# Value projections of two head groups in one 512-column product, half-block scores, and conditioning products in four column groups of the array, in a two-layer hybrid backbone

## The chip, the cores and the metric

The kernel runs on one core of one Trainium2 chip. The metric is the time of one execution on the device, in microseconds (us). A profiled execution of the same kernel gives the trace from which all rows below are taken.

## What is computed

The reference has two layers over 512 latent tokens (and 256 context tokens) of width 1024; all of it is in float32.

```python
m = silu(cvec) @ ada_w + ada_b                      # shift, scale, gate, 1024 each
h = rmsnorm(x) * (1 + scale) + shift                # the same for the context with c_ctx
# layer 0: bidirectional gated linear recurrence, 16 heads of key and value width 128
q, v, zf, zb, gate = split(h @ w_in, 5)             # 2048 columns each
f = lb + (1 - lb) * sigmoid(z); g = log f; k = 1 - f   # forward and backward
S_t = diag(exp g_t) S_{t-1} + k_t^T v_t ; o_t = S_t^T silu(q_t)   # chunks of 16 tokens
x = x + gate_ada * ((rmsnorm(o_f + o_b) * silu(gate)) @ w_out)
# layer 1: gated convolution along the rows of the token grid, norm, gate, projection, final rmsnorm
```

Within a chunk of 16 tokens, and between the chunks of a block of 128 tokens, the output comes from masked scores q k^T (times decay factors) that are multiplied with v; between blocks it comes from states S.

## The kernel before, in words

All activations lie transposed in SBUF (features on partitions). Most products are made precise by a split: each float32 operand becomes a high part and a low part of type fp32r (`split`, L134: ScalarE rounds the high part, VectorE or GpSimd subtracts for the low part), and hi*hi, lo*hi and hi*lo are summed in PSUM, three products for one. Products whose operands are left in plain float32 are issued as two records each, so one float32 matmul is two PE records in the trace.

**Conditioning.** `ada_start` (L144 to L166) makes the shift and scale columns in four steps jj of 512 columns. The stationary operand is the conditioning vector, 2 columns (latent and context) or 4 (high and low), and the 512 weight columns move. `ADA_SPLIT` says which weight pieces are split first (L152 to L156) and which are used in plain float32 (L150). The result, a row of 2 or 4 partitions, is copied (L158) and transposed back into columns by four small products with `sel` (L161). Its weight pieces have six buffers (L230). Between the steps the first five weight pieces of layer 0 are multiplied ("early" products, L248 to L254).

**Layer 0** (L574 to L653) goes over eight groups gi of two heads. For each group TensorE makes forget-gate products (`proj_z`: pz for 512 latent and pc for 256 context tokens, two directions, two heads), query products (pq), value products (pv), output-gate products (pg), and in groups 2, 3 and 5 output products of finished heads (op). A weight piece is 512 KB; its high and low parts have three buffers (L208), and a piece of a buffer that is still read waits for it on ScalarE and VectorE.

`proj_values` (L562) takes two pieces of 256 columns for the two heads of a group. `proj_v` (L307) multiplies them with 6 token tiles (four latent, two context): the tokens are stationary (128 columns), the 256 weight columns move, 8 steps of k with three products each, so 144 records in a group. They stand between the query and the gate products (L582); in the last group between the query products and the recurrence (L595).

`gla` (L329) is the recurrence of one head. Its first part (to the first `yield`, L435) has the gates, running sums, context states (h_ct, h_s, which needs the values), the scaled queries and keys qh and kh, and the block states S. Its second part (L438 to L492) makes the scores: three levels of distance (L439: operands ql and kl on VectorE, then for each of the four 128-token blocks one 128 x 128 float32 product, L465, and one masked copy of 128 x 512 into a1, L466) and two diagonal products (L467 to L475, a1 and a2). So a head has 20 score matmuls and five masked copies. `A` (L477) is their sum; the output products (L484 to L492) follow in one run, and `readout` normalizes. The qh, kh, S tiles have one buffer each, so that heads follow each other there; sg (the gates), qs and gs have two.

**The order** on each engine is chosen when the program is built, by a planner that walks the instructions in program order and fills each engine by estimated times; the chip then runs each engine's list strictly in that order. In the trace the recurrence of a group stands between the forget-gate and query products of the next group.

**Layer 1** (L656 on) has its own products and pools. It shares the weight buffers with layer 0.

Of the kernel before, what the change touches and what calls it, by code (L numbers as in the profile page):

```python
# [9 lines left out]
F32 = mybir.dt.float32  # L10
F32R = mybir.dt.float32r
# [5 lines left out]
P = 128  # L17
D = 1024
KD = D // P
L = 512  # L20
# [15 lines left out]
ADA_SPLIT = ((1, 1, 1, 1), (1, 0, 2, 1), (1, 0, 2, 1), (1, 1, 0, 0))  # L36
# [3 lines left out]
LAST_KQ = 1  # L40
FINAL = ((0, 2, 1), (2, 4, 0), (4, 6, 0))
# [11 lines left out]
C_END = C_TAP + P  # L53
# [7 lines left out]
def hybrid_kernel(ctx: ExitStack, tc: tile.TileContext, xT, ctxT, cvec, consts, norm_g, ada_b, ada_a, ada_c,  # L61
# [63 lines left out]
    sc4 = cpool.tile([P, KD, 4], F32R, name="sc4")  # L125
    V.tensor_copy(out=sc4[:, :, 0:2], in_=sc)
    V.tensor_tensor(out=sc4[:, :, 2:4], in0=sc, in1=sc4[:, :, 0:2].bitcast(F32), op=ALU.subtract)
# [16 lines left out]
    def ada_start(jj, raws, pool, sel):  # L144
        ps = ps_m.tile([P, 512], F32, name=f"adaps{jj}", tag="ms")
        n = 4 if ADA_SPLIT[jj][0] else 2
        for kk, raw in enumerate(raws):
            if not ADA_SPLIT[jj][kk]:
                for k in range(2):
                    mm(ps[0:2], lhsT=sc[:, 2 * kk + k, :], rhs=raw[:, k, :], start=(kk == 0 and k == 0), stop=(kk == 3 and k == 1))  # L150
                continue
            hi, lo = split(pool, raw, [2, 512], f"ada{jj}_{kk}", V if ADA_SPLIT[jj][kk] == 1 else G, ("ahi", "alo"), 2)  # L152
            for k in range(2):
                mm(ps[0:4], lhsT=sc4[:, 2 * kk + k, :], rhs=hi[:, k, :], start=(kk == 0 and k == 0), stop=False)
            for k in range(2):
                mm(ps[0:2], lhsT=sc4[:, 2 * kk + k, 0:2], rhs=lo[:, k, :], start=False, stop=(kk == 3 and k == 1))  # L156
        row = pool.tile([4, 512], F32, name=f"adarow{jj}", tag="adarow", bufs=2)
        V.tensor_copy(out=row[0:n], in_=ps[0:n])  # L158
        pt_ = ps_m.tile([P, 512], F32, name=f"adat{jj}", tag="ms")
        for i in range(4):  # L160
            mm(pt_[:, 2 * i:2 * i + 2], lhsT=row[0:n, i * P:(i + 1) * P], rhs=sel[0:n], start=True, stop=True)  # L161
# [43 lines left out]
    def wpiece(src, shape, name, lo_eng, hi_eng=None):  # L205
        raw = wpool.tile([P] + shape, F32, name=f"{name}_raw", tag="raw")
        nc.sync.dma_start(out=raw, in_=src)
        return split(wpool, raw, shape, name, lo_eng, ("whi", "wlo"), 3, hi_eng)  # L208


    with l0:
# [8 lines left out]
        with tc.tile_pool(name="pinit", bufs=1) as pi:  # L220
            mk = pi.tile([P, 5, P], F32, name="mk")
            eye = pi.tile([4, 4], F32, name="eye")
            nc.gpsimd.dma_start(out=eye, in_=consts[0:4, C_IDN:C_IDN + 4])
            sel = pi.tile([4, 2], F32, name="sel")
            V.tensor_tensor(out=sel, in0=eye[:, 0:2], in1=eye[:, 2:4], op=ALU.add)
# [3 lines left out]
            for jj in range(4):  # L229
                araws.append([pi.tile([P, 2, 512], F32, name=f"ada{jj}_{kk}", tag="araw", bufs=6) for kk in range(4)])  # L230
# [25 lines left out]
            for jj in range(4):  # L256
                ada_start(jj, araws[jj], pi, sel)
# [6 lines left out]
                for i in range(len(early), min(EARLY, len(early) + EARLY_LOADS[jj])):  # L264
                    pool, tags, bufs = (wpool, ("whi", "wlo"), 3) if i < 3 else (pi, ("ehi", "elo"), EARLY - 3)
# [41 lines left out]
        def proj_v(ws, lhi, llo, t, name):  # L307
            ps = ps_p.tile([P, 512], F32, name=name, tag="pj")
            c = slice(t * P, (t + 1) * P)
            for k in range(KD):  # L310
                hi, lo = ws[k // 4]
                mm(ps[:, :256], lhsT=lhi[k][:, c], rhs=hi[:, k % 4, :], start=(k == 0), stop=False)  # L312
                mm(ps[:, :256], lhsT=llo[k][:, c], rhs=hi[:, k % 4, :], start=False, stop=False)  # L313
            for k in range(KD):
                hi, lo = ws[k // 4]
                mm(ps[:, :256], lhsT=lhi[k][:, c], rhs=lo[:, k % 4, :], start=False, stop=(k == KD - 1))
# [12 lines left out]
        def gla(h, j, sg, qs, v):  # L329
# [109 lines left out]
            for lev in (2, 1, 0):  # L439
# [3 lines left out]
                kl = pt.tile([P, L], F32, name=f"{n}_kl{lev}", tag="lk", bufs=2)  # L443
# [4 lines left out]
                else:  # L448
                    ql = pt.tile([P, L], F32, name=f"{n}_ql{lev}", tag="lq", bufs=2)
                    for half in range(2):  # L450
                        dd = [[2 * w, ng_], [CH, hf], [1, CH]]
                        fd = [[2 * hf, ng_], [1, hf], [0, CH]]
                        o, fo = half * w, half * hf + lev * NCH
                        V.tensor_tensor(out=cut(ql, o, dd), in0=cut(qh, o + (1 - half) * L, dd), in1=cut(fac, fo + (1 - half) * 128, fd),
                                        op=ALU.mult)
                        V.tensor_tensor(out=cut(kl, o, dd), in0=cut(kh, o + half * L, dd), in1=cut(fac, 256 + fo + half * 128, fd),
                                        op=ALU.mult)
                p_ = ps_s.tile([P, 512], F32, name=f"{n}_sc{lev}", tag="sc")
                for b in range(NB):
                    bs = slice(b * P, (b + 1) * P)  # L460
                    if lev == 0:
                        qq = cut(qh, L + b * P, [[2 * CH, 4], [CH - L, 2], [1, CH]])
                    else:
                        qq = ql[:, bs]
                    mm(p_[:, bs], lhsT=kl[:, bs], rhs=qq, start=True, stop=True)  # L465
# [108 lines left out]
        for gi in range(8):  # L574
# [4 lines left out]
            if gi < 7:  # L579
# [4 lines left out]
                if gi in OUT_SETS:  # L584
                    out_proj(OUT_SETS[gi])
# [347 lines left out]
```

## Time and profile before

| | us |
|---|---|
| median of 3 runs (lowest, highest) | 1362.88 (1358.25, 1363.73) |
| the profiled execution's own time | 1360.55 |
| its span, first to last instruction | 1358.5 |
| PE busy in the span | 1319.3 |
| VectorE (DVE) busy | 947.6 |
| ScalarE (ACT) busy | 617.5 |
| GpSimd (POOL) busy | 320.1 |

The profiled execution has 2.05 us outside its span. PE's busy time counts each matmul from its start to a modelled end; matmuls overlap, so what one costs is read from the distance of starts. PEld is TensorE loading the stationary operand; it overlaps PE. The granted clock is the share of full speed that the chip gave TensorE.

### The profile page before, as it was taken

The numbers are of one execution on the slowest core, as the hardware profiler recorded it, in microseconds if no ns is written. First come the engines' busy times: TensorE is split into PE (matmuls) and PEld (weight loads), VectorE is DVE, ScalarE is ACT, GpSimd is POOL, SyncE is SP. The second block draws the span as 40 slices with busy tenths as digits, with TensorE's granted clock in tenths as the row PEclk, the third lists the DMA queues.
The fourth block names the chain that finished last, engine by engine and source line by source line (L and its number), as shares of the span: only waits on it lengthen the run. The fifth ranks groups of instructions, "written<-read, shape, count | busy, mean of one in ns | idle before, by whom it ended". The sixth has DMA issues, their size and how long they took to land.

```text
span 1358.5 us, 18696 instructions
## 1 busy us (share of the span) xinstructions
PE 1319.3 (97%) x7396; PEld 1112.0 (82%) x7396; DVE 947.6 (70%) x1496; ACT 617.5 (45%) x932; POOL 320.1 (24%) x291
## 2 busy tenths in 40 slices
PE   6999999999999999999999999999999999999997
PEld 2588888998888898899898888986877777788887
DVE  8868787796687877787668868956467566575223
ACT  6455553553345355455255445525323233375331
POOL 3222241240151132132023124204221211122221
PEclk8999999999999999999999999999999999999999
DMA  9312113114112311312312311213424333222221
GB/s 374 120 62 79 47 63 109 63 47 140 62 48 65 122 47 57 115 35 86 128 32 63 109 47 48 62 45 96 146 82 134 110 94 116 78 78 93 93 78 63
DMA packets 36183, 120.15 MB, mean 88 GB/s; under 512 B 4642, under 2 KB 7106, under 8 KB 36096
## 3 DMA queue, kind: packets, MB, share of 16 engines
q1 hardware_dynamic: 35104, 115.79, 26.0%
q0 software_dynamic: 992, 3.18, 1.0%
q8 instruction: 58, 0.95, 0.3%
q14 instruction: 29, 0.24, 0.1%
HBM read 116.85 MB, written 2.10 MB: 88 GB/s over the span
## 4 chain that ended last, share of the span: by engine, by line
PE 63%; DVE 22%; ACT 5%; DMA 4%; issue 3%; POOL 2%; SPq 0%; DVEq 0%; ACTq 0%
PE pa L702 4%; PE pa L701 4%; PE pa L706 4%; PE pz L301 2%; PE pz L302 2%; PE pz L304 2%; PE cop L843 2%; PE cop L847 2%; PE pgt L770 2%; PE cop L844 2%; PE op L530 2%; DVE adacc L176 2%; PE pgt L768 2%; PE op L532 2%; PE pgt L767 2%
## 5 line engine op out<-in xcount | busy, mean ns | idle before, releaser
L701 PE MATMUL pa<-ci_hi,h_hi 128*128 128x512 f32 x256 | 101.3, 407 | 1.9 <-ACT h_hi L649 1.9
L702 PE MATMUL pa<-ci_lo,h_hi 128*128 128x512 f32 x256 | 101.2, 399 | 0.0
L301 PE MATMUL pz<-h_hi,wz_hi 128*128 128x512 f32 x232 | 93.3, 402 | 0.7 <-ACT wz_hi L139 0.7
L116 POOL TENSOR_SCALAR sg<-sg 128x1536 f32<-128x1536 f32 x16 | 76.6, 4786 | 70.0 <-ACT sg L549 69.8
L302 PE MATMUL pz<-h_lo,wz_hi 128*128 128x512 f32 x232 | 92.9, 401 | 0.0
L176 DVE SCALAR_TENSOR_TENSOR adacc<-adb,sc,adacc 128x128 f32<-128x128 f32 x224 | 76.4, 356 | 3.7
L139 ACT ACTIVATE ci_hi<-ci_raw 128x1024 fp32r<-128x1024 f32 x29 | 30.7, 1060 | 105.9 <-PE pa L706 59.3
L141 POOL TENSOR_TENSOR ci_lo<-ci_raw,ci_hi 128x1024 fp32r<-128x1024 f32 x18 | 44.3, 2464 | 132.8 <-ACT ci_hi L139 105.2
L706 PE MATMUL pa<-ci_hi,h_lo 128*128 128x512 f32 x224 | 72.1, 397 | 0.0
L312 PE MATMUL pv<-wv_hi,h_hi 128*128 128x256 f32 x256 | 63.7, 285 | 0.0
L313 PE MATMUL pv<-wv_hi,h_lo 128*128 128x256 f32 x256 | 63.1, 283 | 0.0
L304 PE MATMUL pz<-h_hi,wz_lo 128*128 128x512 f32 x232 | 61.3, 399 | 0.0
L701 PEld LDWEIGHTS pa<-ci_hi,h_hi 128*128 128x128 f32 x256 | 48.7, 190 | 15.1 <-issue 4.1
L432 DVE SCALAR_TENSOR_TENSOR h_S<-h_S,h_dec,h_kb 128x128 f32<-128x128 f32 x96 | 48.8, 508 | 17.5 <-ACT h_kb L426 16.4
L139 ACT ACTIVATE wz_hi<-wz_raw 128x1024 fp32r<-128x1024 f32 x29 | 30.7, 1058 | 66.1 <-DMA wz_raw<-in_w_in 52.8
L302 PE MATMUL pc<-hc,wz_hi 128*128 128x256 f32 x232 | 59.4, 288 | 0.0
L702 PEld LDWEIGHTS pa<-ci_lo,h_hi 128*128 128x128 f32 x256 | 48.7, 190 | 13.0 <-issue 1.4
L301 PE MATMUL pc<-hc,wz_hi 128*128 128x256 f32 x232 | 59.1, 287 | 0.0
L141 DVE TENSOR_TENSOR wz_lo<-wz_raw,wz_hi 128x1024 fp32r<-128x1024 f32 x29 | 35.4, 1222 | 32.5 <-ACT wz_hi L139 32.3
L400 POOL TENSOR_TENSOR h_f<-h_fac 128x16 f32<-128x16 f32 x16 | 10.1, 628 | 198.5 <-DVE h_kl L446 147.4
L843 PE MATMUL cop<-zhi,co_hi 128*128 128x512 f32 (+1 forms) x160 | 54.2, 352 | 0.0
L377 POOL TENSOR_TENSOR h_ref<-h_tot,h_gt 128x64 f32<-128x64 f32 x16 | 17.5, 1091 | 146.4 <-DVE h_ref L404 136.6
(330 smaller groups left out, 4012.1 us busy)
## 6 DMA issues: line engine op xcount, KB each, us to landing
adb<-in_ada_c SPq DMA_DIRECT2D x32, 512.0 KB, 3.5
ci_raw<-in_c_in SPq DMA_DIRECT2D x32, 512.0 KB, 3.4
wz_raw<-in_w_in SPq DMA_DIRECT2D x29, 512.0 KB, 3.4
ada<-in_ada_a SPq DMA_DIRECT2D x16, 512.0 KB, 6.0
wv_raw<-in_w_v SPq DMA_DIRECT2D x16, 512.0 KB, 3.4
wg_raw<-in_w_in SPq DMA_DIRECT2D x16, 512.0 KB, 3.4
cg_raw<-in_c_gate SPq DMA_DIRECT2D x16, 512.0 KB, 3.4
co_raw<-in_c_out SPq DMA_DIRECT2D x16, 512.0 KB, 3.5
```

The costliest lines, as they stand in the source:

```text
L116: (G if pool_min else V).tensor_scalar(out=t, in0=t, scalar1=EMAX, scalar2=None, op0=ALU.min)
L141: lo_eng.tensor_tensor(out=lo, in0=raw, in1=hi.bitcast(F32), op=ALU.subtract)
L176: V.scalar_tensor_tensor(out=acc, in0=raw[:, k, :], scalar=sc[:, k, 0:1], in1=acc, op0=ALU.mult, op1=ALU.add)
L301: mm(ps[:, :T], lhsT=hi[:, k, :], rhs=rhi[k], start=(k == 0), stop=False)
L302: mm(ps[:, :T], lhsT=hi[:, k, :], rhs=rlo[k], start=False, stop=False)
L304: mm(ps[:, :T], lhsT=lo[:, k, :], rhs=rhi[k], start=False, stop=(k == KD - 1))
L312: mm(ps[:, :256], lhsT=lhi[k][:, c], rhs=hi[:, k % 4, :], start=(k == 0), stop=False)
L313: mm(ps[:, :256], lhsT=llo[k][:, c], rhs=hi[:, k % 4, :], start=False, stop=False)
L701: mm(pss[t], lhsT=h_hi[:, 2 * kq + k, c], rhs=hi[:, k, :], start=(kq == 0 and k == 0), stop=False)
L702: mm(pss[t], lhsT=h_hi[:, 2 * kq + k, c], rhs=lo[:, k, :], start=False, stop=False)
L706: mm(pss[t], lhsT=h_lo[:, 2 * kq + k, c], rhs=hi[:, k, :], start=False, stop=(kq == 3 and k == 1))
L843: mm(ps, lhsT=hi[:, i, c], rhs=zhi[ct][:, tok], start=(ct == 0), stop=False)
```

## The change

- `ada_start` no longer splits. The conditioning vector is padded to 32 columns (`scz`, 2 of them not zero); the eight float32 products of a step write four sets of 32 partitions of one PSUM bank, so each uses 32 of the array's 128 columns. The copy takes 128 partitions, and `sel` (now a [128, 2] constant that is loaded) sums the four sets. The weight pieces have eight buffers.
- Weight high and low parts have four buffers instead of three; four of the five early pieces live there.
- `proj_values` is called in even groups only, behind the gate and output products, for the four heads of two groups, with four pieces of [2, 512] and 512 moving columns: 144 records of 512 columns stand for the 288 of 256 columns of two groups. Both groups' v tiles are made. The context tiles come first.
- For heads 0 to 13 the scores are made in half blocks: each 128 x 128 product is replaced by two of 64 stationary and 64 moving columns that write the upper and lower 64 partitions of PSUM. Level 0 and the two diagonals use the two 64 x 64 blocks on the diagonal; level 1 too, and level 2 fills the other two quarters of the same tile. All operands are made first; three PSUM tiles replace five, one of them from the pool of the transposes; masked copies are six of 64 x 256 and one of 128 x 512. The operand kl of level 0 moves to the buffers of the silu's exponential. Heads 14 and 15 keep whole blocks, with level 1 ahead of level 2.
- The constants get two more columns; the software DMA's scratch is set to 8192 bytes.

```diff
-ADA_SPLIT = ((1, 1, 1, 1), (1, 0, 2, 1), (1, 0, 2, 1), (1, 1, 0, 0))
+W_BUFS = 4
...
             for k in range(2):
-                mm(ps[0:4], lhsT=sc4[:, 2 * kk + k, :], rhs=hi[:, k, :], start=(kk == 0 and k == 0), stop=False)
-            for k in range(2):
-                mm(ps[0:2], lhsT=sc4[:, 2 * kk + k, 0:2], rhs=lo[:, k, :], start=False, stop=(kk == 3 and k == 1))
...
+                c = (2 * kk + k) % 4
+                mm(ps[32 * c:32 * (c + 1)], lhsT=scz[:, 2 * kk + k, :], rhs=raw[:, k, :], start=(kk < 2), stop=(kk >= 2))
+        row = pool.tile([P, 512], F32, name=f"adarow{jj}", tag="adarow", bufs=2)
+        V.tensor_copy(out=row, in_=ps)
...
-        return split(wpool, raw, shape, name, lo_eng, ("whi", "wlo"), 3, hi_eng)
+        return split(wpool, raw, shape, name, lo_eng, ("whi", "wlo"), W_BUFS, hi_eng)
...
-                araws.append([pi.tile([P, 2, 512], F32, name=f"ada{jj}_{kk}", tag="araw", bufs=6) for kk in range(4)])
+                araws.append([pi.tile([P, 2, 512], F32, name=f"ada{jj}_{kk}", tag="araw", bufs=8) for kk in range(4)])
...
-                hi, lo = ws[k // 4]
-                mm(ps[:, :256], lhsT=lhi[k][:, c], rhs=hi[:, k % 4, :], start=(k == 0), stop=False)
-                mm(ps[:, :256], lhsT=llo[k][:, c], rhs=hi[:, k % 4, :], start=False, stop=False)
...
+                hi, lo = ws[k // 2]
+                mm(ps, lhsT=lhi[k][:, c], rhs=hi[:, k % 2, :], start=(k == 0), stop=False)
+                mm(ps, lhsT=llo[k][:, c], rhs=hi[:, k % 2, :], start=False, stop=False)
+                mm(ps, lhsT=lhi[k][:, c], rhs=lo[:, k % 2, :], start=False, stop=(k == KD - 1))
...
+            halves = h < NH - 2
...
+                def half_products(out, col, lhs, rhs):
+                    nonlocal first
+                    for b in range(NB):
+                        for i in range(2):
+                            o = b * P + i * HB
+                            c = col(b, i)
+                            got = mm(out[i * HB:(i + 1) * HB, c:c + HB], lhsT=lhs(o), rhs=rhs(b, i), start=True, stop=True)
+                            first = first or got
+                with nullcontext():
+                    half_products(pz_, lambda b, i: b * HB, lambda o: ops[0][0][:, o:o + HB], lambda b, i: level0_queries(b * P + i * HB, HB))
+                    with tc.issue_after(first.ins):
+                        for d, (t, c0) in enumerate(((pz_, 2 * P), (pd_, 0))):
+                            half_products(t, lambda b, i: c0 + b * HB, lambda o: kh[:, d, o:o + HB],
+                                          lambda b, i: qh[:, d, b * P + i * HB:b * P + (i + 1) * HB])
...
+                for acc, t, c0, m in ((a1, pz_, 0, 0), (a1, pz_, 2 * P, 3), (a2, pd_, 0, 4)):
+                    for i in range(2):
+                        r = slice(i * HB, (i + 1) * HB)
+                        V.copy_predicated(out=cut(acc[r], i * HB, [[P, NB], [1, HB]]), mask=cut(masks[r], m * P + i * HB, [[0, NB], [1, HB]]),
+                                          data=cut(t[r], c0, [[HB, NB], [1, HB]]))
+                masked(a1, px_, 0, 1)
...
-        def proj_values(gi):
-            ws = [wpiece(w_v[gi, kh], [4, 256], f"wv{gi}_{kh}", V) for kh in range(2)]
+        def proj_values(qi):
+            ws = [wpiece(w_v[qi, kq], [2, 512], f"wv{qi}_{kq}", V) for kq in range(4)]
+            vs = [pt.tile([P, 6, 256], F32, name=f"v{qi}_{i}", tag="v", bufs=2) for i in range(2)]
+            for t in (4, 5, 0, 1, 2, 3):
...
-                v = proj_values(gi)
                 gss = [proj_silu(4, gi, j, "g") for j in range(2)]
                 if gi in OUT_SETS:
                     out_proj(OUT_SETS[gi])
+                if gi % 2 == 0:
+                    vs = proj_values(gi // 2)
+                v = vs[gi % 2]
...
-                v = proj_values(gi)
+                v = vs[1]
...
+    nc = _bacc.Bacc("TRN2", target_bir_lowering=False, num_devices=1, dynamic_dma_scratch_size=8192)
```

## Rows read from the trace of the kernel before

**Rows 1.** The page of the kernel before: busy time of the engines (part 1) and the engines' shares in the chain that ended last (part 4).

```profile
PE 1319.3 (97%) x7396; PEld 1112.0 (82%) x7396; DVE 947.6 (70%) x1496; ACT 617.5 (45%) x932; POOL 320.1 (24%) x291
...
PE 63%; DVE 22%; ACT 5%; DMA 4%; issue 3%; POOL 2%; SPq 0%; DVEq 0%; ACTq 0%
```

**Rows 2.** Busy time by stretch: the stretch and its length, then PE, PEld, DVE, ACT and POOL busy (with instructions), the granted clock, the share of the DMA engines and GB/s. 28 to 76 holds the early products; the three from 124, 346 and 556 each hold all projection products of head group 1, 3 or 5, beside the recurrence of the group before it; 840 to 907 is the end of layer 0, 936 the begin of layer 1.

```profile
0.00:28.00 28.00, 15.99 (x38) 4.67 (x39) 21.37 (x32) 18.65 (x25) 12.40 (x11) 0.83 0.94 366
28.00:76.00 48.00, 44.61 (x185) 28.18 (x183) 38.55 (x74) 21.06 (x36) 9.83 (x12) 1.00 0.35 137
...
124.00:227.00 103.00, 98.47 (x638) 87.95 (x637) 80.30 (x133) 51.84 (x83) 26.19 (x28) 1.00 0.23 72
...
346.00:460.00 114.00, 111.78 (x710) 99.55 (x710) 90.67 (x150) 54.23 (x90) 26.81 (x32) 1.00 0.22 70
...
556.00:675.00 119.00, 118.70 (x730) 105.45 (x730) 90.48 (x139) 58.46 (x90) 25.26 (x28) 1.00 0.25 80
...
840.00:907.00 67.00, 66.77 (x458) 61.25 (x457) 53.72 (x92) 33.68 (x57) 9.81 (x13) 1.00 0.17 51
...
936.00:1358.50 422.50, 413.64 (x1852) 329.07 (x1852) 230.56 (x344) 153.00 (x201) 83.72 (x41) 0.99 0.31 97
```

**Rows 3.** PE in order of time (start us, duration us, line, out<-in, form), values of group 5 and, below, gate products of the same group.

```profile
620.79 0.28 PE L312 MATMUL pv<-wv_hi,h_hi 128*128 128x256 f32 x1
...
622.69 1.11 PE L316 MATMUL pv<-wv_lo,h_hi 128*128 128x256 f32 x8
...
639.91 0.39 PE L301 MATMUL pg<-h_hi,wg_hi 128*128 128x512 f32 x1
...
643.63 2.03 PE L304 MATMUL pg<-h_hi,wg_lo 128*128 128x512 f32 x8
```

**Rows 4.** Groups of PE instructions by line and form: the five score products of all heads (count, then busy us and mean ns of one).

```profile
L471 PE MATMUL h_dg<-h_qh,h_kh 128*128 128x128 f32 x256 | 36.5, 276 | 0.3 <-DVE a L466 0.3
...
L465 PE MATMUL h_sc<-h_ql,h_kl 128*128 128x128 f32 x256 | 32.5, 275 | 0.0
...
L465 PE MATMUL h_sc<-h_qh,h_kl 128*128 128x128 f32 x128 | 17.4, 275 | 0.0
```

**Rows 5.** PE in order of time: the scores of one head between context products.

```profile
707.60 1.95 PE L465 MATMUL h_sc<-h_ql,h_kl 128*128 128x128 f32 x16
709.30 0.36 PE L301 MATMUL pc<-hc,wz_hi 128*128 128x256 f32 x1
...
712.18 1.06 PE L465 MATMUL h_sc<-h_qh,h_kl 128*128 128x128 f32 x8
713.07 1.06 PE L471 MATMUL h_dg<-h_qh,h_kh 128*128 128x128 f32 x8
```

**Rows 6.** PE weight loads in order of time: two of 2 columns and one of 128.

```profile
34.10 0.08 PEld L156 LDWEIGHTS adaps<-ada_lo,sc 128*2 128x2 f32 x1 [0.15 <-issue]
34.33 0.19 PEld L251 LDWEIGHTS pe<-h_hi,we_hi 128*128 128x128 f32 x1 [0.15 <-issue]
```

**Rows 7.** PE in order of time, conditioning products (adaps), their transposition (adat) and early products (pe); in brackets the idle time before an instruction and what ended it.

```profile
6.12 1.01 PE L154 MATMUL adaps<-ada_hi,sc 128*4 128x512 f32 x2 [6.12 <-ACT ada_hi L139]
...
13.38 1.05 PE L161 MATMUL adat<-sel,adarow 4*128 4x2 f32 x8 [0.77 <-DVE adarow L158]
...
33.86 0.40 PE L252 MATMUL pe<-h_lo,we_hi 128*128 128x512 f32 x1
34.10 0.64 PE L156 MATMUL adaps<-ada_lo,sc 128*2 128x512 f32 x2
34.57 0.39 PE L251 MATMUL pe<-h_hi,we_hi 128*128 128x512 f32 x1
...
36.66 0.40 PE L253 MATMUL pe<-h_hi,we_lo 128*128 128x512 f32 x1
39.56 1.05 PE L161 MATMUL adat<-sel,adarow 4*128 4x2 f32 x8 [2.50 <-DVE adarow L158]
...
41.55 1.88 PE L150 MATMUL adaps<-ada,sc 128*2 128x512 f32 x4
43.36 0.62 PE L154 MATMUL adaps<-ada_hi,sc 128*4 128x512 f32 x2
...
59.72 0.50 PE L251 MATMUL pe<-h_hi,we_hi 128*128 128x512 f32 x1
```

**Rows 8.** The conditioning products alone, 28 to 76 us: PE, PEld and DVE busy with instructions, granted clock, DMA.

```profile
28.00:76.00 48.00, 12.56 (x39) 2.83 (x38) 2.02 (x3) 1.00 0.35 137
```

**Rows 9.** Groups of instructions by line, engine and form: the splits of the conditioning weights and the largest group of masked copies.

```profile
L466 DVE COPY_PREDICATED a<-masks,h_sc 128x512 f32<-128x512 uint8 x48 | 35.2, 734 | 7.9 <-PE h_sc L465 7.9
...
L141 DVE TENSOR_TENSOR ada_lo<-ada,ada_hi 128x1024 fp32r<-128x1024 f32 x10 | 16.5, 1654 | 3.7 <-ACT ada_hi L139 3.6
...
L139 ACT ACTIVATE ada_hi<-ada 128x1024 fp32r<-128x1024 f32 x12 | 12.5, 1050 | 4.3 <-DMA ada<-in_ada_a 2.7 <-PE adaps L154 1.6
```

**Rows 10.** The end of layer 0: PE's first product of the last value set, the first transposition of the second last head's context keys, and the last state product of the last head.

```profile
839.58 0.28 PE L312 MATMUL pv<-wv_hi,h_hi 128*128 128x256 f32 x1
...
858.46 0.60 PE L354 MATMUL h_ct<-kc,h_ec 128*128 128x128 f32 x4
...
906.65 0.61 PE L491 MATMUL h_o<-h_qh,h_S 128*128 128x128 f32 x4
```

More of the change, by code (lines that the diff above doesn't have):

```diff
@@ L442, in gla @@
                 ng_ = L // (2 * w)
-                kl = pt.tile([P, L], F32, name=f"{n}_kl{lev}", tag="lk", bufs=2)
+                kl = pt.tile([P, L], F32, name=f"{n}_kl{lev}", tag="se" if halves and lev == 0 else "lk", bufs=2)
                 if lev == 0:
@@ L447, in gla @@
                                     in1=cut(f16, 0, [[2, ng_], [1, 2], [0, CH]]), op=ALU.mult)
[L448 to L465, printed above, removed]
-                V.copy_predicated(out=cut(a1, 0, [[P, NB], [1, P]]), mask=cut(masks, lev * P, [[0, NB], [1, P]]), data=cut(p_, 0, [[P, NB], [1, P]]))
@@ L467, in gla @@
-            for d in range(2):
-                p_ = ps_s.tile([P, 512], F32, name=f"{n}_dg{d}", tag="sc")
-                for b in range(NB):
-                    bs = slice(b * P, (b + 1) * P)
-                    mm(p_[:, bs], lhsT=kh[:, d, bs], rhs=qh[:, d, bs], start=True, stop=True)
-                if d == 0:
-                    V.copy_predicated(out=cut(a1, 0, [[P, NB], [1, P]]), mask=cut(masks, 3 * P, [[0, NB], [1, P]]), data=cut(p_, 0, [[P, NB], [1, P]]))
-                else:
-                    V.copy_predicated(out=cut(a2, 0, [[P, NB], [1, P]]), mask=cut(masks, 4 * P, [[0, NB], [1, P]]), data=cut(p_, 0, [[P, NB], [1, P]]))
+                    return kl, None
@@ new lines, in level_operands @@
+                ql = pt.tile([P, L], F32, name=f"{n}_ql{lev}", tag="lq", bufs=2)
+                for half in range(2):
+                    dd = [[2 * w, ng_], [CH, hf], [1, CH]]
+                    fd = [[2 * hf, ng_], [1, hf], [0, CH]]
+                    o, fo = half * w, half * hf + lev * NCH
+                    V.tensor_tensor(out=cut(ql, o, dd), in0=cut(qh, o + (1 - half) * L, dd), in1=cut(fac, fo + (1 - half) * 128, fd),
+                                    op=ALU.mult)
+                    V.tensor_tensor(out=cut(kl, o, dd), in0=cut(kh, o + half * L, dd), in1=cut(fac, 256 + fo + half * 128, fd),
+                                    op=ALU.mult)
@@ L865, in _constants @@
     far = [s // w != t // w for w in (64, 32, 16)]
[L866 removed]
+    for i, m in enumerate((far[2] & ~far[1], far[1], far[0], same & (s <= t), same & (s >= t))):
         k[:, C_MASK + i * P:C_MASK + (i + 1) * P] = m
@@ L885, in _constants @@
     k[:TAPS, C_TAP:C_TAP + NR] = A.T
+    for i in range(2):
+        k[i::32, C_SEL + i] = 1.0
     return k
```

83 lines of the change are left out of this document (49 added, 34 removed).

## The prediction, made before the changed kernel ran

> **What bounds the kernel now.** I read the page's busy times and chain first, then busy time by stretch, then TensorE's list in order of time. TensorE (PE) is busy 97% of the span, and the chain that ended last lies 63% on it [rows 1]. By stretch the picture holds for layer 0 and layer 1: from 28 us on PE has at most a few us of idle time in each stretch, at the full granted clock of 1.00 (2.4 GHz) [rows 2]. Only the first 28 us are different: PE has work for 16 of them, the DMA engines are 0.94 busy and the clock is 0.83 on average. VectorE is the second engine: 80 to 91 us of work in the odd groups' stretches of 103 to 119 us. So PE's time is the kernel's time, as long as nothing else comes to the front. What one PE record costs is the distance from its start to the next, not its duration. A value record of 256 columns costs (622.69 - 620.79) / 16 = 0.119 us, a gate record of 512 columns (643.63 - 639.91) / 16 = 0.2325 us [rows 3]. A float32 score record of 128 columns costs (709.30 - 707.60) / 16 = 0.106 and (713.07 - 712.18) / 8 = 0.111 us [rows 5]; I take 0.108. The counts of the score groups are 256 + 256 + 128 = 640 records, 40 for each of 16 heads [rows 4].
>
> **Scores.** Before, a head costs 40 x 0.108 = 4.3 us of PE. After, it has twice as many records, 80, each with half the stationary and half the moving columns. No row shows such a record or two of them side by side. What bounds today's 0.108 can be seen, though: eight records with 128 stationary but two moving columns take 1.05 us, about 0.115 each, the first transposition [rows 7]. So the weight load alone sets about the same pace as the moving columns do, and both are halved. That loads go by columns is seen in their durations, 0.08 us for 2 columns and 0.19 for 128 [rows 6]. One after another, 80 records then cost 80 x 0.054 = 4.3 us, no gain. The halves of a pair use different columns of the array and different partitions of PSUM, and come in turn in the list; if they run side by side, a head costs 2.2 us. If a record's pace is not set by columns at all but by the instruction, 80 x 0.108 = 8.6 us. So for 14 heads the bounds are 30 us gained and 60 lost. I take the side-by-side value, since both things that are seen to set the pace are halves that do not share columns, less 0.3 us in a head for entering the blocks where the neighbour is a full-width product: 1.8 x 14 = **25 us gained**.
>
> A change of shape may cost more than that. In the trace, a 2-column product between full-width ones starts 0.24 us after the record ahead of it, two records of it take 0.47 us, and the next full-width record follows at the usual pace (33.86 to 34.57) [rows 7]: no pause at either change. The Trainium skill, TensorEngine Tiling (Array Packing), section Key Properties, says that changing the tiling mode drains TensorE, and also that different tiles load and multiply in parallel. The row speaks against the first statement if the narrow product counts as another mode; no run here yet shows the second. By the first, each change would cost something in this kernel, and that is a rival below.
>
> VectorE's masked copies cost 0.734 us for 512 columns [rows 9]. Five become one of 512 and six of 256, which at half the columns are about 0.4 us: 3.1 for 3.7 us. That is off the path, since PE covers it; it helps only where VectorE would come to the front. The level-0 operand in the silu's buffers adds a wait of the silu on level-0 scores, which come first in their block, and the diagonal tile in the transposes' pool delays a key transposition at most by its masked copies (below 1 us); both lie under the next group's 512-column products. If that cover is gone they count among the stalls below.
>
> **Values.** 8 x 144 = 1152 records at 0.119 us are 137.1 us; 576 at 0.2325 are 133.9: **3 us gained**. Splits, loads (16 pieces) and ScalarE copies (48) stay as many. Two waits are new. The four pieces hold all four weight buffers, so the next piece's split waits for the last token tile; its first k-pair is read 1.4 us into that tile's 24 x 0.2325 = 5.6 us, so some 4 us are left for a split of 1.05 us on ScalarE and at most 1.65 on VectorE, as splits of that size take [rows 9]. And both v tiles are written at once, so ScalarE's copies wait for the odd group's last head to finish reading. Behind the ScalarE queue then wait the other PSUM copies, and PE after three tiles. The gate products (11 us by 48 x 0.2325) lie between and cover it.
>
> **What the move uncovers.** The value products are also cover for the recurrence. In odd groups PE loses 144 x 0.119 = 17.1 us of them and 2 x 2.1 us of scores. The stretch of group 1 falls from 103 to 82 us, with 80.3 us of VectorE work less about 4 (split and copies); group 3 from 114 to 93 with 90.7 less 4; group 5 from 119 to 98 with 90.5 less 4 [rows 2]. VectorE then has 93% of the first two; the even groups give slack to catch up. I take 2 us of stall in each of the first two, 4 in all; bounds 0 and 15. At the end of layer 0 the values of the last group (839.58 to 858.46) cover the start of the last two heads, which run from there to about 907 [rows 10]. They go away; left for PE in that stretch are 67 - 17 = 50 us against 53.7 us of VectorE work, less up to 3.3 for the two value splits [rows 2]. So 1 to 17 us come out as stall, and I take 4, since VectorE was not full before and some of its work can start sooner. Together **8 us lost**.
>
> **Conditioning.** Its splits leave ScalarE (12.5 us) and VectorE (16.5 us) [rows 9], work that lies in the first 60 us. On PE, split records of 512 columns become float32 records, which cost (43.36 - 41.55) / 4 = 0.45 us [rows 7]; 16 of them in a step. From 28 to 76 us the conditioning products now take some 12 us [rows 8]. Two steps in that stretch would cost 14.4 us one after another, 3.6 with four side by side; but two records of one product share their columns and follow each other, so pairs, 7.2, is nearer. That saves 5 us, and some of the idle time such as the 2.5 us ahead of 39.56 [rows 7] goes as well. I take **7 us gained**. The ends: one after another loses 9 us (2.4 here, the rest in the first step, which at the low level of the clock, 1.2 GHz and 0.9 us a record, would take 14 us instead of 13.38 - 0.77 - 6.12 = 6.5 [rows 7]); four side by side with no idle time and a start 3 us sooner gains 15. The first loads stay, and so does their bound of about 28 us.
>
> At nothing I cost: the padded vector, the new `sel` constant (needed at 13.4 us, issued at the begin), the eight loading buffers, the order of levels in heads 14 and 15, and the smaller DMA scratch (its loads are used behind products of layer 1; uncovered, a few us).
>
> **Sum.** 25 + 3 + 7 - 8 = 27 us off the profiled execution's 1360.55 (span 1358.5 and 2.05 around it) gives 1333.6. The median of the runs is 2.3 us above that execution, so the forecast is **1336 us**.
>
> **Rivals.** *Halves one after another* (the other side). Place: the array in the score blocks and the conditioning steps. Scores gain nothing, the conditioning loses 6, values gain 3, stalls cost 8: 11 us slower, 1374. It decides from the score record's price: with the rest as here, the kernel is slower once a half record costs over (4.3 - 11/14) / 80 = 0.044 us. For it: no row shows two products at once, and today every record starts after the one ahead has streamed. Against: they share no columns. Chance 0.20. *The cover was needed*: the recurrence becomes the bound in odd groups and at the end, 24 us of stalls instead of 8: 1352. For it, VectorE's 93%; against, a chain of 22% on VectorE that PE mostly covers. 0.17. *A pause at each change of shape*, at a score record's duration less its pace, 0.276 - 0.108 = 0.168 us [rows 4]: five blocks a head are ten changes, 140 for 14 heads, 23 us less the 4 counted: 1355. 0.06, as the narrow products show none. *The order goes wrong*: the planner's times fit the new products badly and scatter the halves among full-width ones, so that few pairs meet: scores gain half, 1348, or less. 0.05.
>
> **How the numbers follow.** Forecast 0.52. What can be told from no change here is 0.5%, 6.8 us. Faster: forecast, most of the cover rival, half of the scattered and paused ones, 0.69; within 0.5% 0.12; slower 0.19, nearly all from the halves in sequence. The range goes from 1318 (scores 30, conditioning 13, stalls 1) to 1375 (halves in sequence); the forecast's own is 1322 to 1348.
>
> **What would show it.** Right: score records in pairs with about 0.03 us from start to start; value records 0.23 us apart; PE idle in some places at the end of layer 0 and in group 1; the early products over by some 68 us instead of 76. Wrong: score records 0.05 us or more apart, gaps of 0.1 us and more at block borders, or PE idle time of over 20 us with VectorE as releaser.

## The result and the profile after

The changed kernel takes **1372.6 us** (median of 5 runs, 1371.7 to 1377.8) for 1362.9 before: the ratio is 1.0088 (95% interval 1.0062 to 1.0113). It is slower by some 10 us where 27 us less were forecast. The profiled execution took 1371.73 us; its mean granted clock is 0.973, for 0.993 before.

The page of the changed kernel, busy time and chain, answers to [rows 1]:

```profile
PE 1299.7 (95%) x7380; PEld 1066.9 (78%) x7380; DVE 928.7 (68%) x1513; ACT 608.8 (44%) x920; POOL 312.9 (23%) x289
...
PE 71%; DVE 16%; ACT 5%; DMA 3%; issue 2%; POOL 2%; SPq 0%; DVEq 0%; ACTq 0%; POOLq 0%
```

PE's busy time fell by 19.6 us, and yet the span grew by 11.3: its idle time is 1369.8 - 1299.7 = 70 us, for 39 before. The chain does not show it: VectorE has less of it than before. The stretches do (columns as in [rows 2]; 133 to 227.6 is group 1, 365.5 to 465.8 group 3, 846 to 950.1 the end of layer 0, the last one layer 1):

```profile
28.00:69.00 41.00, 37.80 (x171) 25.18 (x169) 27.54 (x62) 14.68 (x29) 7.21 (x11) 0.96 0.43 166
133.00:227.60 94.60, 82.10 (x595) 71.42 (x594) 77.00 (x138) 48.32 (x76) 25.32 (x30) 0.93 0.19 62
...
365.50:465.80 100.30, 93.67 (x631) 78.81 (x626) 83.00 (x145) 49.65 (x79) 25.78 (x30) 0.97 0.20 64
...
846.00:950.10 104.10, 87.73 (x434) 68.59 (x433) 74.12 (x124) 45.82 (x75) 26.34 (x23) 0.89 0.17 52
950.10:1369.80 419.70, 408.64 (x1852) 328.83 (x1852) 225.92 (x343) 152.65 (x199) 82.98 (x40) 0.99 0.31 96
```

Group 1 has 12.5 us of idle time, group 3 6.6 and the end 16.4, where [rows 2] have 4.5, 2.2 and (up to 907 us) 0.2. The granted clock is 0.93, 0.97 and 0.89 in them, where it was 1.00 in all three. A clock of 0.89 over 104 us means that about 23 us passed at 1.2 GHz instead of 2.4. By the mean clocks, (1 - 0.973) x 1369.8 x 2 = 74 us of the execution were at the low level, for 19 before (estimates from the mean).

**What TensorE waited for** (releaser, us in all, times, longest):

```profile
PE op L562 <- ACT h_oh L549: 13.2, 4, 4.8
PE h_pp L416 <- ACT h_kb L413: 5.9, 6, 2.9
...
PE adbps L170 <- DVE adacc L168: 4.8, 1, 4.8
PE wtp L676 <- DMA dw<-in_c_dw: 4.0, 1, 4.0
PE pa L737 <- ACT h_hi L685: 3.6, 1, 3.6
```

The largest is new: the output products read `h_oh`, the readout of a head whose recurrence has just ended. Before, the value products of the group stood ahead of them beside the gate products; now only the gate products do. PE in order of time, group 2:

```profile
305.65 0.40 PE L564 MATMUL op<-h_oh,wo_lo 128*128 128x512 f32 x1
308.39 0.73 PE L562 MATMUL op<-h_oh,wo_hi 128*128 128x512 f32 x2 [2.34 <-ACT h_oh L549]
309.89 0.79 PE L562 MATMUL op<-h_oh,wo_hi 128*128 128x512 f32 x1 [0.77 <-DVE gs L312]
310.48 0.63 PE L563 MATMUL op<-h_ol,wo_hi 128*128 128x512 f32 x1
310.91 0.63 PE L564 MATMUL op<-h_oh,wo_lo 128*128 128x512 f32 x1
...
312.19 0.63 PE L564 MATMUL op<-h_oh,wo_lo 128*128 128x512 f32 x1
312.62 0.47 PE L562 MATMUL op<-h_oh,wo_hi 128*128 128x512 f32 x1
312.92 0.39 PE L563 MATMUL op<-h_ol,wo_hi 128*128 128x512 f32 x1
```

PE waits, and the records behind the wait come 0.43 us apart instead of 0.23 until the clock is back (here by 312.9). The same is seen in group 3 behind a wait of 4.8 us that ends at 447. At the end of layer 0 two waits and the slow records behind them follow each other:

```profile
917.07 1.02 PE L539 MATMUL h_ms<-h_sq,ones 128*128 128x512 f32 x2
922.05 3.73 PE L676 MATMUL wtp<-dw,tap 31*118 31x512 f32 x4 [3.97 <-DMA dw<-in_c_dw]
927.89 1.65 PE L562 MATMUL op<-h_ohl,wo_hi 128*128 128x512 f32 x3 [2.10 <-ACT h_ohl L549]
929.34 0.63 PE L563 MATMUL op<-h_ohl,wo_hi 128*128 128x512 f32 x1
929.76 0.63 PE L564 MATMUL op<-h_ohl,wo_lo 128*128 128x512 f32 x1
```

In group 1 VectorE's passes over the later conditioning columns (`adacc`, the wait of 4.8 us above) hold up the recurrence. The raw buffers that they read also hold SP's queue, which loads the weights (start, us held). Four loads of these columns take it 38.55 us, and the next group's weights are asked for at 223.04 only:

```profile
181.23 38.55 SPq L164 DMA_DIRECT2D adb<-in_ada_c  x4
223.04 0.33 SPq L199 DMA_DIRECT2D wz_raw<-in_w_in  x1
```

In the kernel before the four loads behind this group took 8.35 us:

```profile
212.10 8.35 SPq L172 DMA_DIRECT2D adb<-in_ada_c  x4
```

What the held queue cost TensorE directly is small, though. Its first product of group 2 waited 0.72 us for these weights:

```profile
227.65 0.80 PE L294 MATMUL pz<-h_hi,wz_hi 128*128 128x512 f32 x1 [0.72 <-ACT wz_hi L137]
```

**What went as forecast.** The half records do run side by side. PE in order of time, scores of one head (answers to [rows 5]):

```profile
163.61 0.33 PE L474 MATMUL h_s0d<-h_qh,h_kl 128*64 128x64 f32 x2
163.87 0.50 PE L544 MATMUL h_ms<-h_ol,ones_r 128*128 128x512 f32 x1
164.30 0.62 PE L474 MATMUL h_s0d<-h_qh,h_kl 128*64 128x64 f32 x13
164.70 0.22 PE L474 MATMUL h_s0d<-h_qh,h_kh 128*64 128x64 f32 x1
164.75 0.22 PE L474 MATMUL h_s0d<-h_qh,h_kl 128*64 128x64 f32 x1
164.76 0.62 PE L474 MATMUL h_s0d<-h_qh,h_kh 128*64 128x64 f32 x14
165.17 0.22 PE L474 MATMUL h_sx<-h_ql,h_kl 128*64 128x64 f32 x1
```

From 164.30 to 165.17 stand 13 + 1 + 1 + 14 = 29 records: 0.030 us each, for 0.108 of a whole record before. By the trace's start times they come in pairs 6 to 7 ns apart, a pair every 0.058 us. But entering and leaving such a block costs: the h_ms record at 163.87, ahead of one, holds PE for 0.43 us where a 512-column record takes 0.23, and two half records alone (163.61) take 0.26 us. The planner has spread the 1120 half records over 59 such blocks, which take 46 us in all, with the waits inside them.

The values' records (first fence, with lines left out: 12 records in 2.73 us, 0.2275 each) and the conditioning products of 28 to 69 us (second fence: 6.13 us for the 12.56 of [rows 8]) also came out near their prices. The early products are over at 68.1 us, for 75.5.

```profile
333.62 0.39 PE L305 MATMUL pv<-wv_hi,hc 128*128 128x512 f32 x1
...
336.35 0.39 PE L305 MATMUL pv<-wv_hi,hc 128*128 128x512 f32 x1
```

```profile
28.00:69.00 41.00, 6.13 (x32) 0.99 (x32) 1.37 (x2) 0.96 0.43 166
```

### The profile page after: what moved, and what is told of

Same layout as the page of the kernel before. It is cut to its first block, busy times and chain, and to the rows that moved or that the text cites. A ratio compares the mean times of both kernels' runs of the same rounds, so it can differ in the third digit from the quotient of the medians.

```text
span 1369.8 us, 18604 instructions
## 1 busy us (share of the span) xinstructions
PE 1299.7 (95%) x7380; PEld 1066.9 (78%) x7380; DVE 928.7 (68%) x1513; ACT 608.8 (44%) x920; POOL 312.9 (23%) x289
## 4 chain that ended last, share of the span: by engine, by line
PE 71%; DVE 16%; ACT 5%; DMA 3%; issue 2%; POOL 2%; SPq 0%; DVEq 0%; ACTq 0%; POOLq 0%
PE pa L737 4%; PE pa L738 4%; PE pa L742 4%; PE pv L307 3%; PE pv L305 3%; PE pv L306 3%; PE pz L294 3%; PE pz L295 3%; PE pz L297 3%; PE cop L879 2%; PE cop L883 2%; PE cop L880 2%; PE py L776 2%; PE op L562 2%; PE pgt L803 2%
## 5 line engine op out<-in xcount | busy, mean ns | idle before, releaser
L168 DVE SCALAR_TENSOR_TENSOR adacc<-adb,sc,adacc 128x128 f32<-128x128 f32 x224 | 82.9, 384 | 3.5
L423 DVE SCALAR_TENSOR_TENSOR h_S<-h_S,h_dec,h_kb 128x128 f32<-128x128 f32 x96 | 55.5, 580 | 35.1 <-ACT h_kb L417 33.9
L509 POOL TENSOR_TENSOR h_A<-a,a 128x512 f32<-128x512 f32 x16 | 36.8, 2303 | 133.7 <-DVE a L490 121.3
L562 PE MATMUL op<-h_oh,wo_hi 128*128 128x512 f32 x112 | 48.0, 437 | 14.4 <-ACT h_oh L549 13.2
L368 POOL TENSOR_TENSOR h_ref<-h_tot,h_gt 128x64 f32<-128x64 f32 x16 | 13.8, 864 | 175.6 <-DVE h_ref L395 175.4
L294 PEld LDWEIGHTS pz<-h_hi,wz_hi 128*128 128x128 f32 x232 | 44.2, 191 | 9.5 <-ACT wz_hi L137 1.1
L803 PE MATMUL pgt<-h_hi,cg_hi 128*128 128x512 f32 x128 | 51.1, 399 | 0.0
```

The lines of the kernel that those rows point to most:

```text
L168: V.scalar_tensor_tensor(out=acc, in0=raw[:, k, :], scalar=sc[:, k, 0:1], in1=acc, op0=ALU.mult, op1=ALU.add)
L294: mm(ps[:, :T], lhsT=hi[:, k, :], rhs=rhi[k], start=(k == 0), stop=False)
L562: mm(ps, lhsT=hi[:, i, c], rhs=og[h][0], start=(i == 0), stop=False)
L803: mm(ps, lhsT=w[0][:, k, :], rhs=h_hi[:, k, :], start=(k == 0), stop=False)
```

## Experiments

The kernel before took 1362.3 to 1363.8 us beside each set of runs, so times are compared across sets to about 1.5 us. "Four buffers" are the weight buffers of the change.

| run | halves | conditioning | values | buffers | us | ratio to before (95%) |
|---|---|---|---|---|---|---|
| the change | new | new | new | 4 | 1372.6 | 1.0062 to 1.0113 |
| values_back | new | new | old | 4 | 1339.2 | 0.9811 to 0.9849 |
| values_only | old | old | new | 4 | 1411.3 | 1.0339 to 1.037 |
| halves_only | new | old | old | 4 | 1358.9 | 0.9956 to 0.9986 |
| cond_only | old | new | old | 4 | 1352.4 | 0.9907 to 0.9937 |
| place_256 | new | new | old form, new place | 4 | 1378.0 | 1.0094 to 1.0124 |
| end_old | new | new | new; groups 6, 7 old | 4 | 1364.5 | 1.0001 to 1.0019 |
| **values_back_w3** | new | new | old | 3 | **1326.8** | 0.9717 to 0.9755 |
| before_pad | old | old | old | 3 | 1355.7 | 0.9933 to 0.9962 |
| in_group_w3 | new | new | old, behind the gates | 3 | 1343.9 | 0.984 to 0.9879 |
| halves_only_w3 | new | old | old | 3 | 1345.8 | 0.9835 to 0.989 |
| place_256_w3 | new | new | old form, new place | 3 | 1383.4 | 1.012 to 1.0165 |

Three more runs, on the later conditioning columns, stand in the text below.

Theory: the moved values were cover, and the place costs what the trace shows as waits. Rivals: their form does; the halves don't bring what they seem to; the buffers do it.

**Which part loses.** values_back takes `proj_v`, `proj_values`, their calls and the layout of `w_v` back to those of before; the other three put one part of the change into the kernel before, with four buffers.

```diff
+                v = proj_values(gi)
                 gss = [proj_silu(4, gi, j, "g") for j in range(2)]
                 if gi in OUT_SETS:
                     out_proj(OUT_SETS[gi])
-                if gi % 2 == 0:
-                    vs = proj_values(gi // 2)
-                v = vs[gi % 2]
...
-                v = vs[1]
+                v = proj_values(gi)
```

Expected of values_back:

> The changed kernel with the value products of before: two heads at a time, 256 columns, between the query and the gate products, in the last group ahead of the recurrence; half-block scores, conditioning in column groups and four weight buffers stay. Theory 'the values were cover': the stalls of the changed kernel (about 59 us over what its TensorE work explains, from the stretches of its trace) go, and the half scores (some 30 us) and conditioning (7 us) remain: 1322 to 1330 us. Rival 'the scores make the stalls' (all operands first, more and smaller masked copies, one tile in the transposes' pool): the stalls stay and only the few us of the wider value products are lost: 1365 us or more. Third, the four buffers or the other small edits cost time: in between.

Of values_only:

> The kernel before with the value products of the change alone (four heads, 512 columns, behind the gate and output products in even groups, four weight buffers), with whole-block scores and split conditioning. Theory 'the values were cover': slower than before by 15 to 45 us, 1378 to 1408 us, with TensorE idle in group 1, at the output products of groups 2, 3 and 5 and at the end of layer 0. Rival 'the scores make the stalls': within 5 us of before or some us faster, 1356 to 1364.

Of halves_only:

> The kernel before with the half-block scores and four weight buffers alone. Theory 'the values were cover': 14 heads by 4.3 - 2.0 us is 32 us of TensorE time and most of it shows: 1330 to 1338 us. Rival 'the scores make the stalls': the recurrence gets later and the saved TensorE time turns to idle time: 1355 us or slower.

Of cond_only:

> The kernel before with the conditioning products in column groups and four weight buffers alone. Both theories: the early products end some 7 us sooner and nothing else changes, 1354 to 1358 us. If the buffers or the smaller edits cost something, it shows here as a time of 1360 or more although the early products end sooner.

The values with four buffers cost 48.6 us, 3 more than the range that I gave, and without them the change gains 23.5: the loss is theirs, though values_back stays some 10 us short of its forecast. The halves alone missed theirs by over 20 us, and landed where the rival "the scores make the stalls" had them; values_back (1339.2 for the rival's 1365 or more) rules that rival out all the same. The theory as it stood explains neither shortfall; the runs with three buffers below explain most of both. The conditioning gained a little more than forecast (the address, below).

**Place or form.** place_256 makes the old 256-column products of both groups in the new place (`proj_values` and `proj_v` are those of before):

```diff
                 if gi % 2 == 0:
-                    vs = proj_values(gi // 2)
+                    vs = [proj_values(gi), proj_values(gi + 1)]
```

> The changed kernel with the value products in their old form (256 columns, two pieces for each group, 288 records for two groups) but in the new place: both groups' values behind the gate and output products of the even group. Theory that the place is the cause (the odd groups and the end of layer 0 lose their cover): about the changed kernel's 1372.6 plus the 3 us that the wide form saved, 1368 to 1382 us. Rival, that the form is the cause (four pieces that hold all four weight buffers, two tiles of values written at once): near the kernel with the old values, 1339 to 1348.

1378.0: the place alone costs 1378.0 - 1339.2 = 39 us, and the wide form gains 5.4 over it. The rival is out. Since both kernels have the same products, their pages also part the cost (place_256, then values_back; spans 1376.2 and 1337.7):

```profile
PE 1307.7 (95%) x7956; PEld 1097.8 (80%) x7956; DVE 932.0 (68%) x1513; ACT 609.9 (44%) x920; POOL 313.8 (23%) x289
```

```profile
PE 1290.7 (96%) x7956; PEld 1088.0 (81%) x7956; DVE 933.9 (70%) x1513; ACT 607.1 (45%) x920; POOL 309.3 (23%) x289
```

Of the 38.5 us between the spans, 21.5 are idle time (68.5 for 47.0), and 17.0 are the same 7956 records taking longer, at a mean clock of 0.976 for 0.990.

**Where.** end_old leaves groups 6 and 7 their old values (`proj_values2`, 256 columns); the end of layer 0 is covered again.

```diff
+                if gi == 6:
+                    v = proj_values2(gi)
...
-                if gi % 2 == 0:
+                if gi % 2 == 0 and gi < 6:
                     vs = proj_values(gi // 2)
-                v = vs[gi % 2]
+                if gi < 6:
+                    v = vs[gi % 2]
...
-                v = vs[1]
+                v = proj_values2(gi)
```

> The changed kernel with groups 6 and 7 having their value products of 256 columns in their old places; groups 0 to 5 keep the new ones. Theory that the loss is stalls where the cover went, some 25 of 59 us of them at the end of layer 0: 1345 to 1353 us. Rival, that the loss comes in the odd groups alone (VectorE's work there) and the end only shows what was late already: 1364 to 1372.

1364.5, 8 us gained: the number that the rival gave, but not for its reason, since the end itself is cured. Its stretch is now this, 96 us at a clock of 0.99 with 4.4 us more of PE's busy time, where the change took 104 at 0.89:

```profile
846.00:942.00 96.00, 92.14 (x534) 76.01 (x532) 70.45 (x116) 46.56 (x80) 23.20 (x20) 0.99 0.21 65
```

But all of this comes later. TensorE begins group 6 at 678.67 us in the change and at 684.06 in end_old, though the code of groups 0 to 5 is the same:

```profile
678.67 0.50 PE L294 MATMUL pz<-h_hi,wz_hi 128*128 128x512 f32 x1
```

```profile
684.06 0.50 PE L294 MATMUL pz<-h_hi,wz_hi 128*128 128x512 f32 x1
```

So the 8 us are a balance. From there to the first product of layer 1 the change takes 271.6 us and end_old 258.4, 13 less; 5.4 were lost in groups 3 to 5, for a reason that wasn't traced. The end is still the smaller part of the 39 us, and the 20 and more that I gave it were too many.

in_group_w3 leaves each group its values and only puts them behind its gate and output products (three buffers, as values_back_w3):

```diff
-                v = proj_values(gi)
                 gss = [proj_silu(4, gi, j, "g") for j in range(2)]
                 if gi in OUT_SETS:
                     out_proj(OUT_SETS[gi])
+                v = proj_values(gi)
```

> The kernel with three weight buffers and the old values (1326.75), with one move: each group's value products stand behind the gate and output products of their own group instead of ahead of them. Each odd group keeps its values; what is uncovered is the readout of the head that the output products read. Theory that the move within the group already costs these waits (some 10 us of idle time and as long at the slow clock): 1338 to 1348 us. Rival, that only the move out of the odd groups costs: 1325 to 1330.

1343.9, 17 us slower than 1326.8, as the theory said: the readout that the output products read is uncovered by this small move alone. Its waits, which values_back_w3 doesn't have:

```profile
PE op L564 <- ACT h_oh L551: 8.8, 3, 4.9
...
PE op L564 <- DVE gs L314: 3.6, 3, 2.4
```

**VectorE's later columns.** ada_even was meant to take the later conditioning columns out of the bare groups:

```diff
-            for col in range(*((0, 4, 8, 12, 15, 18, 21, 24, 24)[gi:gi + 2])):
+            for col in range(*((0, 0, 8, 8, 16, 16, 24, 24, 24)[gi:gi + 2])):
```

> The changed kernel with the 24 later conditioning columns (a 512 KB load, eight VectorE passes and a small product each) made in other groups' parts: 8 each behind groups 1, 3 and 5, none behind 0, 2, 4, 6 and 7, so that the stretches that lost the values have none. Theory that in group 1 their VectorE work (four columns, some 12 us) and their loads, which hold the weight queue, make up most of that group's 12 us of idle time and of the slow clock behind it: 1355 to 1364 us, group 1 at 82 to 88 us instead of 94. Rival, that the recurrence alone is too long for the bare group: 1368 to 1376, group 1 at 92 or more.

1461.3 us (ratio 1.0692 to 1.0738): a miss by 100 us. The columns behind group 1 fall into the end of that group's stretch, which has no values; eight in one lump took 135 us instead of 94 there. It does show how they hurt: of SP's queue, 72 us in one wait for VectorE's passes, in a stretch whose VectorE work is 109 us beside 104 of PE at 0.88.

```profile
SPq L164 <- DVE adacc L168: 88.3, 5, 72.0
```

```profile
134.00:269.00 135.00, 104.12 (x771) 89.92 (x770) 108.98 (x214) 57.00 (x95) 28.48 (x34) 0.88 0.15 47
```

So the columns were left out instead (range(24, 24) in every group, constants in their place, so the output is not the reference's), in the changed kernel and in values_back_w3:

> The changed kernel with the 24 later conditioning columns of layer 0 left out (their loads, 192 VectorE passes of 0.38 us, 24 small products; constants stand for them, so the output is not the reference's). Beside the kernel with the old values and three buffers, cut in the same way. Theory that VectorE's and the weight queue's load makes the bare groups late: below 1340 us, that is less than 20 us above the other. Rival, that the recurrence's own chain and the readouts do: 1355 to 1368 us, 35 to 46 above the other.

> The kernel with the old values and three weight buffers (1326.75), without the 24 later conditioning columns of layer 0 (the same work left out). Both theories: where TensorE is covered, this work is off the path but for 24 x 4 small records and 2 us of waits, so 1310 to 1325 us.

1332.1 and 1310.7 us. The distance falls from 45.9 to 21.4 us, between the two theories and nearer to the first: about half of what the change loses against the better kernel comes from VectorE's passes and their loads meeting the bare groups. The other half is left for the readouts, the recurrence, the end and the fourth buffer, which the better kernel doesn't have; these runs don't part them. The two parts aren't independent, either: without the columns the waits for the readouts fall from 13.2 to 4.6 us.

```profile
PE op L563 <- ACT h_oh L550: 4.6, 4, 1.7
```

Group 1 in the changed kernel without the columns:

```profile
134.00:206.00 72.00, 71.87 (x486) 62.36 (x485) 58.95 (x88) 41.35 (x63) 20.78 (x20) 1.00 0.18 58
```

Idle time gone, clock 1.00, VectorE at 82% of the stretch.

**The fourth buffer.** `W_BUFS = 3` in values_back:

> The changed kernel with the value products of before and three weight buffers instead of four. Theory that the fourth buffer costs some 5 us (every kernel with four has 6 us of idle time on TensorE in layer 1, the kernel before 2.4): 1333 to 1336 us. Rival, that the buffers are worth nothing either way: 1338 to 1341; that the fourth buffer was a gain that hid elsewhere: 1343 or more.

1326.8: 12.5 us faster, more than twice what I expected, and the best complete kernel of the study, 2.6% faster than before. Part of the cost is seen where layer 1 begins. ScalarE in values_back (four buffers), then PE's first product of layer 1:

```profile
913.00 0.69 ACT L678 ACTIVATE r_rs<-r_ss,eps 128x512 f32<-128x512 f32 x1 [1.58 <-PE r_ss L663]
913.59 1.05 ACT L137 ACTIVATE ci_hi<-ci_raw 128x1024 fp32r<-128x1024 f32 x1
914.53 0.62 ACT L679 ACTIVATE r_rs<-r_rs 128x512 f32<-128x512 f32 x1
```

```profile
918.50 0.76 PE L735 MATMUL pa<-ci_hi,h_hi 128*128 128x512 f32 x1 [3.64 <-ACT h_hi L683]
```

And in values_back_w3:

```profile
903.86 0.69 ACT L678 ACTIVATE r_rs<-r_ss,eps 128x512 f32<-128x512 f32 x1 [2.20 <-PE r_ss L663]
904.58 0.63 ACT L679 ACTIVATE r_rs<-r_rs 128x512 f32<-128x512 f32 x1
```

```profile
907.59 0.69 PE L735 MATMUL pa<-ci_hi,h_hi 128*128 128x512 f32 x1 [1.86 <-ACT h_hi L683]
```

With four buffers the planner has put a weight split (1.05 us) between the two steps of the norm for which PE waits, and the wait is 3.64 us for 1.86. That is some 2 of the 12.5 us. Another 2 are a longer wait for ScalarE within layer 1 (2.5 us for 0.6), but there a split stands ahead in both kernels, so it isn't shown to be the split. The rest lies in layer 0 and wasn't traced. The same buffer in two other kernels:

```diff
-W_BUFS = 4
+W_BUFS = 3
```

> The kernel before with half-block scores alone and three weight buffers (with four it took 1358.9). Theory that the halves gain about 16 us of TensorE's time (46 instead of 62 us for 14 heads) and that the fourth buffer took 12 of them back: 1345 to 1349 us. Rival, that the planner's scattering of the halves takes the gain whatever the buffers: 1355 to 1360.

> The kernel with the old 256-column form in the new place (1378.0 with four weight buffers), with three. If the place and the fourth buffer cost independently (39 and 12 us over 1326.75): 1363 to 1368 us. If the stalls of the place hide what the buffer costs: 1374 to 1380; if three buffers make the eight value pieces late: 1382 or more.

The halves with three buffers take 1345.8: 17.9 us less than the kernel before, and 13 less than the halves with four. In the trace the half records now stand in 52 blocks of 42 us, where whole ones took 14 x 4.3 = 60: the same 18 us. With the values moved the sign turns: 1383.4 with three, 5.4 more than with four. So the place costs 57 us with three buffers and 39 with four. That is the number of the last of the three cases that I had written down, late value pieces; of its reason one wait is seen:

```profile
PE pv L309 <- DVE wv_lo L139: 2.1, 1, 2.1
```

The rest of the 5.4 us stays open.

**The address.** Records that read h cost 0.227 us in kernels with the new conditioning and 0.232 in the others. With the vector `sc4` gone, the weight buffers lie 128 bytes off their old place (in steps of 256 bytes it is the same to which side). before_pad only makes that vector 128 bytes longer, and the second half of it is unused:

```diff
-    sc4 = cpool.tile([P, KD, 4], F32R, name="sc4")
...
+    sc4 = cpool.tile([P, 2 * KD, 4], F32R, name="sc4")
...
```

> The kernel before with 128 bytes more in each partition ahead of the weight buffers, nothing else. The 512-column records whose operand is h cost 0.227 us in the kernels with the new conditioning and 0.232 in the others, and in the first the weight buffers lie 128 bytes further. Theory that the address sets this: records at 0.227 us, some 2700 x 0.0047 = 12 us faster, 1349 to 1353 us. Rival, that it is something else of the new conditioning or of the order: 1360 to 1365, records at 0.232.

1355.7, 7.3 us faster, with 0.228 instead of 0.232 us a record; 12 was too high. Layer 1 (its row of [rows 2] has 422.50 and 413.64):

```profile
937.00:1353.60 416.60, 407.68 (x1852) 328.63 (x1852) 230.77 (x344) 152.98 (x200) 83.29 (x41) 0.99 0.32 98
```

The same 1852 records take 5.9 us less. That a shift by 128 bytes does it is shown; which pair of addresses matters is not.

## Why the prediction was wrong

From kernel to kernel, the change is: halves 1363.7 to 1345.8 (-17.9); conditioning, with the shift of addresses, to 1326.8 (-19.1); the fourth buffer to 1339.2 (+12.5); the place to 1378.0 (+38.8); the wide form to 1372.6 (-5.4). Against my terms:

- **What the move uncovers** was the step that failed: 8 us forecast, 39 measured (57 with three buffers). I priced the cover by shares: VectorE at 93% of a stretch still fits, so 2 us a group. The share came out (77.0 us of VectorE beside 82.1 of PE in group 1, 94%), and yet 12.5 us of that stretch were idle: a share says nothing of order. What came out were single waits: readouts that the output products read next (13.2 us in all, in none of my terms), a pass over a column load (4.8 us at once), the end of layer 0. And the records behind the long waits ran at 1.2 GHz; I had counted no clock at all. By place_256 against values_back, 21.5 us of waiting brought 17.0 us of slower records, so each us of waiting was paid about 1.8 times.
- **The fourth buffer** had no price: the prediction names it only as what the value pieces hold. With the values in their place it cost 12.5 us.
- **Scores**: the mechanism was right, the size off: 18 us for 25. The record costs 0.029 us, near the 0.027 taken; but I allowed 0.3 us a head for entering the blocks (4 us), and there are 52 to 59 blocks, at (42 - 1120 x 0.029) / 52 = 0.18 us each, some 10 us. The Trainium skill, TensorEngine Tiling (Array Packing), section Key Properties, says both things that I weighed: that a change of tiling mode drains the engine, and that tiles load and multiply in parallel. These runs agree with both (0.18 us a block; 0.030 us a record, where 0.054 was reckoned for one after another); the 2-column products from which I argued against the first [rows 7] are no guide to half blocks.
- **Values** (3 forecast, 5.4 measured) and **conditioning** (7 forecast, 7.4 in the early products) were right. Of the values' 5.4 some 3 are the address: 576 records at 0.2275 us for the 0.2325 taken. Of the 19.1 that came with the conditioning 7.3 are the address, which no row of before could show, and some 4 stay open.

Of the rivals, halves in sequence, the one on the slower side, is out; that its 1374 us stand next to the measured 1372.6, and that the time lies within the wide range, is chance. (In that rival the conditioning loses 6 us, where its own paragraph has 9; the sum would be 1377.) "The cover was needed" had the mechanism, at 24 us, too small to change the sign. Scattering and a pause at the borders of a block are both real and together worth most of the 7 us that the scores lack.

All four signs of being right came true, since each looked at one part by itself. The sign of a missing cover looked for VectorE as releaser; the largest single releaser is ScalarE's `h_oh`.

## What to carry to other kernels

A block of independent products on the bounding engine is also what hides the chains beside it: before moving it, list what each next product reads and when that is ready, and count the engine's slower clock behind every new wait as well as the wait. Buffers are not free either where a planner fills strict lists: with one more it put work ahead of what the bounding engine waits for (shown for some 2 of 12.5 us here). Change such things one at a time; here two gains of 18 and 19 us were hidden by one move and one buffer.

## What the runs showed that was not expected

- Two half-width float32 records start 6 to 7 ns apart and a pair goes every 58 ns; each such block costs about 0.18 us beyond its records.
- 128 bytes of offset of the weight buffers are worth 4 to 5 ns on a 512-column record, 7.3 us of this kernel.
- Behind waits of 2.3 to 4.8 us on PE records came 0.43 us apart instead of 0.23 (310 to 312 us, 449 us, behind 927): the low level of the clock. The same 7956 records took 17 us longer with 21.5 us more of waits among them.
- One more weight buffer cost 12.5 us with the values in their place and gained 5.4 with them moved.
